# Filler bytes that shift where two tiles start in SBUF

## The chip, the cores and the metric

The kernel runs on one core of a Trainium2 chip. The metric is device time in microseconds (us) of one execution; the figure of a kernel is the median of its runs.

## The reference

The reference is two blocks of transformer-like layers on a sequence of 256 tokens with 1024 features, in float32. Each weight is used once, on all 256 tokens:

```python
for l in range(2):                     # first block
    h = hybrid_mixer(x, ...)           # x @ w_in (7680 columns), two attentions, a convolution, gates, w_mix_out
    x = layer_norm(alpha * x + h, ...)
    h = memory_cross_attention(x, mem, xa_q, xa_kv, xa_o)   # 256 memory tokens
    x = layer_norm(alpha * x + h, ...)
    h = conv_ffn(x, ...)               # x @ ffn_w_in (2 * 2816 columns), gating, @ ffn_w_out
    x = layer_norm(alpha * x + h, ...)
for l in range(2):                     # second block
    x = x + 0.5 * swiglu(norm(x), ...) # 1024 -> 2 * 2816 -> 1024
    x = x + mixer2(norm(x), ...)       # x @ w_in_2, two attentions, a convolution, a pooling, @ w_out_2
    x = x + 0.5 * swiglu(norm(x), ...)
```

## The kernel before, in words

All weights come from one packed array, in the order of use, as 674 halves of 128 x 1024 floats (512 KB). SP loads each into one of five staging tiles `stg`. A float32 product is made of three fast ones: ACT rounds the half to the format fp32r (`wh`, 8 buffers), DVE takes the rest `stg - wh` (`wl`, 7 buffers), the activations are split likewise, and TensorE adds high x high, low x high and high x low into PSUM. These products are nearly all of its work.

A TensorE product has a stationary operand of 128 x 128, which a weight load brings in, and a moving operand, which streams past it. There are three kinds of product here.

- `chunk_A`, lines 385 to 387: a piece of `wh` or `wl` is stationary, and 256 columns of activations move. The activations are `xT`, the normalised input of a layer transposed (8 chunks, high and low, 256 tokens; one tile, used by every layer), `memT`, the memory tokens in the same form, or pairs of 2 x 256 from `ring`.
- `group_B` and `group_Bt`, lines 423 to 425 and 445 to 452: a piece of `xT` or `memT` (128 tokens) is stationary, and 512 columns of `wh` or `wl` move.
- `run_BK`, lines 478 to 480 and 503: a piece of a `ring` pair is stationary, and 512 columns of `wh` or `wl` move. These are the projections at the end of each part.

The order is written out by hand: `weight_order` fixes the order of the halves, and the generator emits the instructions of side work (attention, convolution) between them. The change does not touch it.

Tiles lie in each of SBUF's 128 partitions one behind the other, pool after pool in the order in which the pools are made (`stg`, `wh`, `wl`, `one`, `xT`, a `gap`, `ring`, `tmp`, `sm`, and then those of `first`: `memT`, `KT` and small ones). Every tile is rounded up to 32 bytes. Only the first address of each pool is of interest here, taken modulo 256 bytes; all buffers of a pool and all slices that TensorE reads of these tiles are multiples of 256 bytes apart:

| tile | before | after |
|---|---|---|
| `stg`, `wh`, `wl` | 128 | 128 |
| `xT` | 32 | 64 |
| `ring`, `tmp` | 128 | 128 |
| `memT`, `KT` | 128 | 64 |
| `nab` (a mask, in attention) | 192 | 128 |

Quoted once, the pools around `xT`, in the kernel before:

```python
self.p_xT = P("xT", 1)
P("gap", 1).tile([128, 24], F32, name="gap")
self.p_ring = P("ring", 23)
```

Of the kernel before, what the change touches and what calls it, by code (L numbers as in the profile page):

```python
# [11 lines left out]
F32 = mybir.dt.float32  # L12
# [218 lines left out]
class Gen:  # L231
    def __init__(self, nc, tc, T, ctx):
        self.nc, self.tc, self.T, self.ctx = nc, tc, T, ctx
        P = lambda name, bufs, **k: ctx.enter_context(tc.tile_pool(name=name, bufs=bufs, **k))
        self.p_stg = P("stg", 5)
        self.p_hl = P("wh", NHL)
        self.p_wl = P("wl", NHL - 1)
        self.p_one = P("one", 1)
        self.p_xT = P("xT", 1)

        P("gap", 1).tile([128, 24], F32, name="gap")
        self.p_ring = P("ring", 23)
        self.p_tmp = P("tmp", 8)
        self.p_sm = P("sm", 24)
        PS = bass.MemoryType.PSUM
        self.p_acc = P("acc", 4, space=PS)
        self.p_tp = P("tp", 4, space=PS)
        self.used = 0
        self.n = 0
        self.cur = 0  # L250
        self.n_dma = 0
        self.n_h = 0
        self.n_l = 0
        self.stg = {}
        self.hl = {}
        self.lead = 4
        self.floor = None
        self.sides = []
        self.later = []
        self.early = []  # L260
# [556 lines left out]
    def setup(self):  # L817
        nc, T = self.nc, self.T
        one = self.p_one
        self.xn = one.tile([128, 2, D], F32, name="xn")  # L820
        self.ident = one.tile([128, 128], F32, name="ident")
        self.mhalf = one.tile([128, 8], F32, name="mhalf")
        self.cols = one.tile([128, N_COLS], F32, name="cols")
        self.lam = one.tile([128, DEPTH], F32, name="lam")
        self.subg = one.tile([128, DEPTH, 128], F32, name="subg")
        self.cs2 = one.tile([128, 2, 2, 16], F32, name="cs2")
        self.c1 = one.tile([128, 200], F32, name="c1")

    def first(self, ctx):
        nc, T = self.nc, self.T  # L830
        pf = ctx.enter_context(self.tc.tile_pool(name="first", bufs=1))
        pna = ctx.enter_context(self.tc.tile_pool(name="na", bufs=2))
        memT = pf.tile([128, 8, 2, 256], F32R, name="memT")
        KT = pf.tile([128, 8, 256], F32, name="KT")
        mraw = [self.ring([128, 2, 256]) for _ in range(4)]
        for k in range(4):
            nc.sync.dma_start(mraw[k], T["memT"][:, 2 * k:2 * k + 2, :])
            if k == 0:
                self.dma_w()
        for _ in range(3):  # L840
            self.dma_w()

        def load_x(t):
            for c in range(2):
                nc.sync.dma_start(self.halves(t)[c], T["x"][t * 128:t * 128 + 128, c * 512:c * 512 + 512])

        load_x(0)
        self.dma_w()
        g0, b0 = self.bcast_rows(T["emb_ln_g"], D, nc.sync), self.bcast_rows(T["emb_ln_b"], D, nc.sync)
        load_x(1)  # L850
        self.trig = pf.tile([128, 4, 2, 8], F32, name="trig")
        self.posf = pf.tile([128, 2], F32, name="posf")
        self.posi = pf.tile([128, 2], I32, name="posi")
        nc.gpsimd.memset(self.mhalf, -0.5)
        make_identity(nc, self.ident)
        self.memT, self.KT = memT, KT
        for k in range(4):
            self.split_to(memT[:, 2 * k:2 * k + 2, 0, :], memT[:, 2 * k:2 * k + 2, 1, :], mraw[k])
            if k == 0:
                self.pump(0, 0)  # L860

        def emb(t):
            list(self.ln_chain(self.halves(t), g0, b0))

        self.lead = 2
        self.xk(0, range(1))
        emb(0)
        nc.sync.dma_start(self.c1, T["c1"])
        nc.sync.dma_start(self.cols, T["cols"])
        lamr = self.lamr = self.ring([128, 2, 4, 64])  # L870
        nc.sync.dma_start(lamr, T["lamr"].partition_broadcast(128))
        nc.sync.dma_start(self.subg, T["subln_g"].partition_broadcast(128))
        nc.sync.dma_start(self.posi, T["pos"])
        self.xk(0, range(1, 2))
        xT = self.new_xT()
        self.transpose_in(0, self.halves(0), xT)
        self.lead = 3
        self.xk(0, range(2, 3))
        emb(1)
        self.lead = 4  # L880
        self.xk(0, range(3, 4))
        tr1 = self.turn1(self.halves(1), xT)
        for l in range(DEPTH):
            xT, tr1 = self.mixer1(l, xT, tr1, pna)
            xT, tr1 = self.cross(l, xT, tr1)
            if l == 0:
                self.sides.append(self.small_setup2())
            xT, tr1 = self.ffn1(l, xT, tr1)
        return xT, tr1
# [421 lines left out]
    def swiglu(self, l, which, xT, tr1, gap, final=False):  # L1311
# [21 lines left out]
        for j in range(2, NFF):  # L1333
            ps = self.chunk_A(("UG", n, l, j), x, pool=self.acc if j < NFF - 2 else self.tp)
            if j == 2:
                first()
            s, p = self.tmp([128, 256]), self.pair()
            nc.scalar.activation(s, ps[:, 1, :], AF.Silu)  # L1338
            nc.vector.tensor_tensor(s, ps[:, 0, :], s, op=ALU.mult)  # L1339
            self.split_to(p[:, 0, :], p[:, 1, :], s)  # L1340
            hT.append(p)
# [251 lines left out]
```

## Time and profile before

| | |
|---|---|
| median of 3 runs | 2063.93 us (2063.58 to 2064.59) |
| profiled execution, its own time | 2066.26 us |
| its span (first to last instruction) | 2064.5 us |
| PE, PEld busy | 99%, 90% |
| DVE, ACT busy | 63%, 53% |
| matmuls | 14064 |
| moved by DMA | 376.89 MB, 183 GB/s |

PE is TensorE's matmuls and PEld its weight loads; both overlap. The duration that the profile gives a matmul runs from its start to the end of its way through the array, and the next one starts long before that. What a matmul costs in a dense stretch is the distance from its start to the next start.

### The profile page before, as it was taken

What the parts mean: (1) busy time and instruction counts of PE and PEld (TensorE: products, weight loads), DVE (VectorE), ACT (ScalarE), POOL (GpSimd) and SP (SyncE); (2) the same over time, 40 slices, a digit from 0 to 9 for tenths busy, and PEclk for the clock granted to TensorE, in tenths of its full rate; (3) what the DMA queues carried; (4) which work ended last, traced back from release to release, by engine and by line L of the source; (5) the groups of instructions that cost most, each with busy time, mean ns of one, the idle gap of its engine ahead of it and who ended that gap; (6) DMA issues with size and microseconds to landing.
All of it is one profiled execution on the core that took longest, in us unless ns stands there. A gap on an engine that the chain in (4) does not pass through costs nothing.

```text
span 2064.5 us, 34809 instructions
## 1 busy us (share of the span) xinstructions
PE 2038.1 (99%) x14064; PEld 1864.0 (90%) x14064; DVE 1302.5 (63%) x2001; ACT 1091.1 (53%) x1798; POOL 96.8 (5%) x142
## 2 busy tenths in 40 slices
PE   8999999999999999999999999999999999999998
PEld 7899988899888999989987998879998998879996
DVE  6776674877577657457766555776555555676553
ACT  5757445465375644536553544575444544574442
POOL 2100000000010000000001000100000000100000
PEclk9999999999999999999999999999999999999999
DMA  7544664466564565545564656555564656545562
GB/s 287 189 152 164 200 215 137 144 208 200 184 204 135 172 205 175 190 136 187 187 240 158 205 184 223 159 160 174 184 220 147 206 187 222 162 152 179 186 216 72
DMA packets 105522, 376.89 MB, mean 183 GB/s; under 512 B 12560, under 2 KB 12816, under 8 KB 105232
## 3 DMA queue, kind: packets, MB, share of 16 engines
q1 hardware_dynamic: 99936, 357.85, 52.4%
q0 software_dynamic: 5136, 16.29, 2.9%
q8 instruction: 110, 1.80, 0.4%
q10 hardware_dynamic: 288, 0.52, 0.1%
q14 instruction: 52, 0.43, 0.1%
HBM read 372.49 MB, written 1.05 MB: 181 GB/s over the span
## 4 chain that ended last, share of the span: by engine, by line
PE 92%; DVE 4%; issue 1%; DMA 1%; POOL 1%; ACT 1%; SPq 0%; POOLq 0%; DVEq 0%
PE acc L385 17%; PE acc L386 16%; PE acc L387 16%; PE acc L480 6%; PE acc L478 6%; PE acc L479 6%; PE acc L503 4%; PE acc L423 3%; PE acc L425 3%; PE acc L424 3%; PE acc L452 1%; PE acc L447 1%; PE acc L445 1%; PE tp L387 1%; PE tp L385 1%
## 5 line engine op out<-in xcount | busy, mean ns | idle before, releaser
L320 DVE TENSOR_TENSOR wl<-stg,wh 128x1024 fp32r<-128x1024 f32 x670 | 801.5, 1223 | 187.8 <-PE acc L479 111.1
L308 ACT CAST wh<-stg 128x1024 fp32r<-128x1024 f32 (+1 forms) x673 | 683.9, 1047 | 177.2 <-PE acc L480 121.1
L385 PE MATMUL acc<-xT,wh 128*128 128x256 f32 x2624 | 740.7, 282 | 0.6 <-ACT xT L597 0.6
L386 PE MATMUL acc<-xT,wh 128*128 128x256 f32 x2624 | 736.2, 281 | 0.7 <-DVE xT L598 0.7
L387 PE MATMUL acc<-xT,wl 128*128 128x256 f32 x2624 | 736.1, 281 | 0.0
L385 PEld LDWEIGHTS acc<-xT,wh 128*128 128x128 f32 x2624 | 494.5, 188 | 3.3 <-ACT xT L597 1.1
L386 PEld LDWEIGHTS acc<-xT,wh 128*128 128x128 f32 x2624 | 494.6, 188 | 1.7 <-DVE xT L598 1.1
L387 PEld LDWEIGHTS acc<-xT,wl 128*128 128x128 f32 x2624 | 494.4, 188 | 0.0
L478 PE MATMUL acc<-wh,ring 128*128 128x512 f32 x528 | 207.3, 393 | 0.0
L480 PE MATMUL acc<-wh,ring 128*128 128x512 f32 x528 | 205.8, 390 | 0.2
L479 PE MATMUL acc<-wl,ring 128*128 128x512 f32 x528 | 205.6, 389 | 0.0
L480 PEld LDWEIGHTS acc<-wh,ring 128*128 128x128 f32 x528 | 99.1, 188 | 21.7 <-DVE ring L519 1.1
L478 PEld LDWEIGHTS acc<-wh,ring 128*128 128x128 f32 x528 | 99.1, 188 | 20.6 <-issue 0.3
L503 PE MATMUL acc<-wh,ring 128*128 128x512 f32 x384 | 117.5, 394 | 0.0
L479 PEld LDWEIGHTS acc<-wl,ring 128*128 128x128 f32 x528 | 99.2, 188 | 20.1
L1339 DVE TENSOR_TENSOR tmp<-acc,tmp 128x256 f32<-128x256 f32 x72 | 30.5, 424 | 137.2 <-ACT tmp L1338 137.2
L1338 ACT ACTIVATE tmp<-acc 128x256 f32<-128x256 f32 x72 | 27.7, 385 | 164.9 <-PE acc L387 164.9
L515 ACT CAST ring<-tmp 128x256 fp32r<-128x256 f32 x136 | 54.7, 407 | 87.2 <-DVE tmp L1246 42.0
L516 DVE TENSOR_TENSOR ring<-tmp,ring 128x256 fp32r<-128x256 f32 x136 | 57.3, 425 | 64.1 <-ACT ring L515 64.1
L503 PEld LDWEIGHTS acc<-wh,ring 128*128 128x128 f32 x384 | 72.1, 188 | 14.2
L539 POOL TENSOR_TENSOR sm<-sm,mhalf 128x1 f32<-128x1 f32 (+1 forms) x40 | 31.6, 790 | 1032.6 <-DVE sm L550 413.0
L423 PE MATMUL acc<-wh,xT 128*128 128x512 f32 (+1 forms) x192 | 75.3, 392 | 0.0
(235 smaller groups left out, 2649.7 us busy)
## 6 DMA issues: line engine op xcount, KB each, us to landing
stg<-in_wpack SPq DMA_DIRECT2D x673, 512.0 KB, 4.2
nab<-in_rpb POOLq DMA_DIRECT2D x8, 384.0 KB, 3.9
ring<-in_ln_g POOLq DMA_DIRECT2D x12, 256.0 KB, 3.7
ring<-in_ln_b POOLq DMA_DIRECT2D x12, 256.0 KB, 4.8
ring<-in_ffn_norm POOLq DMA_DIRECT2D x8, 256.0 KB, 4.3
cst<-hpad POOLq DMA_DIRECT2D x32, 32.9 KB, 4.1
ring<-in_memT SPq DMA_DIRECT2D x4, 256.0 KB, 5.5
xn<-in_x SPq DMA_DIRECT2D x4, 256.0 KB, 7.5
```

The lines of the kernel that those rows point to most:

```text
L308: self.nc.scalar.copy((h.bitcast(F32) if f32 else h)[:, c:c + w], self.stg[i][:, c:c + w])
L320: (self.nc.gpsimd if i in POOL_LOW else self.nc.vector).tensor_sub(l, s, self.hl[i][0].bitcast(F32))
L385: mm(out, lh, rh, start=start, stop=False)
L386: mm(out, lh, rl, start=False, stop=False)
L387: mm(out, ll, rh, start=False, stop=stop)
L423: mm(o, xp[:, 0, ts], h[:, w], start=(i == 0), stop=False)
L424: mm(o, xp[:, 0, ts], l[:, w], start=False, stop=False)
L425: mm(o, xp[:, 1, ts], h[:, w], start=False, stop=(i == n - 1))
L478: mm(b[t][c], xp[:, 0, ts], h[:, w], start=(i == 0), stop=False)
L479: mm(b[t][c], xp[:, 0, ts], l[:, w], start=False, stop=False)
L480: mm(b[t][c], xp[:, 1, ts], h[:, w], start=False, stop=False)
L503: mm(b[tt][cc], xp[:, 1 if kind == "x" else 0, ts], l[:, w] if kind[0] == "l" else h[:, w], start=False, stop=(kind == "x" and i == n - 1))
```

## The change

Four lines. The tile `c1` is made 32 bytes longer and used as before, which shifts `xT` by 32 bytes. The unused tile `gap` behind `xT` shrinks by 32 bytes, so that `ring` and all that follows it in the same pools stay where they are. A new unused tile `gap1` of 192 bytes ahead of `memT` shifts `memT`, `KT` and the small tiles behind them by 192 bytes. On each engine the same instructions stand in the same order, on tiles of the same names; only addresses differ.

```diff
--- before.py
+++ after.py
@@ -238,7 +238,7 @@
         self.p_one = P("one", 1)
         self.p_xT = P("xT", 1)
 
-        P("gap", 1).tile([128, 24], F32, name="gap")
+        P("gap", 1).tile([128, 16], F32, name="gap")
         self.p_ring = P("ring", 23)
         self.p_tmp = P("tmp", 8)
         self.p_sm = P("sm", 24)
@@ -824,12 +824,13 @@
         self.lam = one.tile([128, DEPTH], F32, name="lam")
         self.subg = one.tile([128, DEPTH, 128], F32, name="subg")
         self.cs2 = one.tile([128, 2, 2, 16], F32, name="cs2")
-        self.c1 = one.tile([128, 200], F32, name="c1")
+        self.c1 = one.tile([128, 208], F32, name="c1")[:, :200]
 
     def first(self, ctx):
         nc, T = self.nc, self.T
         pf = ctx.enter_context(self.tc.tile_pool(name="first", bufs=1))
         pna = ctx.enter_context(self.tc.tile_pool(name="na", bufs=2))
+        pf.tile([128, 48], F32, name="gap1")
         memT = pf.tile([128, 8, 2, 256], F32R, name="memT")
         KT = pf.tile([128, 8, 256], F32, name="KT")
         mraw = [self.ring([128, 2, 256]) for _ in range(4)]
```

## Rows read from the trace of the kernel before

**Rows 1.** The page: busy time, share of the span, instructions.

```profile
PE 2038.1 (99%) x14064; PEld 1864.0 (90%) x14064; DVE 1302.5 (63%) x2001; ACT 1091.1 (53%) x1798; POOL 96.8 (5%) x142
```

**Rows 2.** What PE waited for: total us, times, longest us.

```profile
PE acc L385 <- ACT wh L308: 5.4, 1, 5.4
...
PE acc L387 <- DVE wl L320: 2.4, 2, 1.9
...
PE acc L386 <- DVE xT L598: 0.7, 2, 0.3
PE acc L385 <- ACT xT L597: 0.6, 2, 0.3
...
PE acc L447 <- DVE wl L320: 0.3, 1, 0.3
PE acc L445 <- ACT xT L597: 0.2, 1, 0.2
```

**Rows 3.** Tile xT, its matmuls of 256 columns; duration in ns.

```profile
L385 PE MATMUL acc<-xT,wh x2624: 277/281/472, 47.5 to 1982.5; 128*128 128x256 f32 x188
...
L385 PE MATMUL tp<-xT,wh x192: 277/281/283, 490.6 to 1993.9; 128*128 128x256 f32 x192
```

**Rows 4.** Tile xT, matmuls that hold a piece of it.

```profile
L423 PE MATMUL acc<-wh,xT x192: 278/394/503, 72.3 to 1838.3; 128*128 128x512 f32 x160, 128*128 128x256 f32 x32
...
L445 PE MATMUL acc<-wh,xT x160: 388/394/793, 34.7 to 1875.9; 128*128 128x512 f32 x160
```

**Rows 5.** Tile memT, its matmuls, one row of three each.

```profile
L385 PE MATMUL acc<-memT,wh x128: 274/283/580, 5.4 to 875.8; 128*128 128x256 f32 x128
...
L423 PE MATMUL acc<-wh,memT x64: 387/389/582, 289.0 to 897.3; 128*128 128x512 f32 x64
```

**Rows 6.** Timeline of PE from 817.2 us, first and last of 15.

```profile
817.23 0.28 PE L385 MATMUL acc<-memT,wh 128*128 128x256 f32 x1
...
818.91 0.28 PE L387 MATMUL acc<-memT,wl 128*128 128x256 f32 x1
```

**Rows 7.** Windows in long stretches of xT: engines' busy us, instructions.

```profile
core 0: us, PE busy (x) PEld busy (x) DVE busy (x) ACT busy (x) POOL busy (x), PEclk, DMA share, GB/s
395.00:485.00 90.00, 90.00 (x761) 90.00 (x760) 69.54 (x128) 55.78 (x91) 0.58 (x1) 1.00 0.59 191
...
1610.00:1700.00 90.00, 90.00 (x770) 90.00 (x769) 50.98 (x66) 43.91 (x65) 0.00 (x0) 1.00 0.59 188
```

**Rows 8.** Timeline of PE from 316.8 us, first and last of 19.

```profile
316.77 0.28 PE L387 MATMUL acc<-xT,wl 128*128 128x256 f32 x1
...
318.93 0.28 PE L387 MATMUL acc<-xT,wl 128*128 128x256 f32 x1
```

**Rows 9.** A window in the down projection, ring as stationary operand.

```profile
1250.00:1300.00 50.00, 50.00 (x222) 41.39 (x222) 24.59 (x22) 19.91 (x20) 0.14 (x1) 1.00 0.70 227
```

**Rows 10.** Timeline of PE from 296.3 us, first and last of 12.

```profile
296.30 0.39 PE L425 MATMUL acc<-wh,memT 128*128 128x512 f32 x1
...
298.80 0.39 PE L424 MATMUL acc<-wl,memT 128*128 128x512 f32 x1
```

**Rows 11.** Timeline of PE from 1594.8 us, equal neighbours merged.

```profile
1594.80 1.79 PE L445 MATMUL acc<-wh,xT 128*128 128x512 f32 x7
1596.43 2.03 PE L447 MATMUL acc<-wl,xT 128*128 128x512 f32 x8
1598.30 1.09 PE L452 MATMUL acc<-wh,xT 128*128 128x512 f32 x4
```

**Rows 12.** Groups of PE by line: matmuls on the ring.

```profile
L478 PE MATMUL acc<-wh,ring 128*128 128x512 f32 x528 | 207.3, 393 | 0.0
...
L503 PE MATMUL acc<-wh,ring 128*128 128x512 f32 x384 | 117.5, 394 | 0.0
L503 PE MATMUL acc<-wl,ring 128*128 128x512 f32 x192 | 68.9, 389 | 0.0
...
L385 PE MATMUL acc<-ring,wh 128*128 128x256 f32 x192 | 54.7, 285 | 0.0
```

## The prediction

> **What bounds the kernel now.** I read the page first, then the waits of TensorE, then the matmuls by form, then the distance between the starts of neighbouring matmuls. The page gives PE 99% busy, PEld 90%, DVE 63%, ACT 53% [rows 1]. A busy PE is little evidence, since matmuls are pipelined; the waits say it better: what PE waits for other engines comes to 15.5 us of 2064.5 in ten rows from 5.4 to 0.2 [rows 2]. So the kernel lasts as long as 14064 matmuls take one behind the other, and the number to read is what one takes from its start to the next start, the slot. The duration of one (282 ns) is longer than its slot and isn't the cost.
>
> Seven matmuls in ten involve the tiles that move. 8448 matmuls stream 256 columns of xT past a 128x128 piece of wh or wl (3 x 2624 + 3 x 192) [rows 3]. 960 hold a piece of xT and stream 512 columns of wh or wl [rows 4]. memT does the same in 384 and 192 instructions [rows 5].
>
> **What the slots are.** The diff moves no instruction; it moves start addresses. So I look for places where one shape runs at different distances between its operands' addresses modulo 256 bytes. I write the distance as moving minus stationary.
> - Distance 0, 256 columns: memT against wh and wl. 14 slots between the two rows shown, 1.68 us, 120.0 ns each [rows 6].
> - Distance -96 (xT at 32, weights at 128): in six long stretches of several hundred matmuls a window of 90 us holds 761 of them (in four more windows 760 or 761) and 770 once [rows 7]. A window counts what overlaps it, so I divide 90.28 us by the count: 118.6 ns five times, 117.2 ns once. Same code, same data sizes, two patterns. A shorter stretch of cross attention ran a third one, 18 slots in 2.16 us, 120.0 ns [rows 8].
> - Distance 0, 512 columns: 50.39 us by 222 instructions, 227.0 ns (ring as stationary) [rows 9]; memT as stationary 11 slots in 2.50 us, 227.3 ns [rows 10].
> - Distance +96, 512 columns, xT as stationary: 7 slots in 1.63 us, then 8 in 1.87 us, 233.3 ns [rows 11].
>
> At distance 0 the second 256 columns cost 227 - 120 = 107 ns, 0.417 ns a column, which is 2.4 GHz; the granted clock in the windows was 1.00 of that [rows 7]. So 256 columns alone are 106.7 ns and every slot holds something more: 13.3 ns at distance 0 in both shapes (32 columns' time), 11.9 or 10.5 ns at -96, 20.0 ns at +96 (48 columns). 32 and 48 are two and three times 16 columns, and 16 columns of four bytes are 64 bytes. In the patterns at -96 the loss is 28.6 and 25.2 columns, about 1.8 and 1.6 of such pieces. My reading: while one stationary operand is loaded and another is streamed, the two reads meet a few times, and each meeting costs the time of 64 bytes. At a start that lies on 64 bytes (0) the count is whole and steady; at 32 bytes beside it (-96) it is broken and depends on how a stretch happened to begin.
>
> The Trainium skill speaks against this: "SBUF — State Buffer", section "SBUF: two separate sides", says that TensorE has ports of its own and never waits on anyone; "TensorE: Matmul & The Clock Gate", section "Step-by-step: what each phase is for", says that loading the next weights doesn't steal read bandwidth from the running matmul. By that rule the change is worth nothing and the time stays at 2063.9; by the rows, as summed below, it falls by 13. The trace disagrees with it at 120.0 against 117.2 ns and 227.0 against 233.3 ns for the same shapes.
>
> **The change part by part.**
> - xT goes from -96 to -64 as moving operand, from +96 to +64 as stationary one; memT and KT from 0 to -64. The ring's gap shrinks by what c1 and xT grew, so the ring, tmp and what lies behind stay where they were: 2160 slots of 227 ns on the ring as stationary operand (3 x 528 + 384 + 192) and 3 x 192 on it as moving one don't change [rows 12].
> - Nothing is added: the fillers are never written, c1 is still used as 200 columns. KT's 64 matmuls in scores and the writes of xT by ACT and DVE shift with their tiles; I put them at nothing, as PE's whole wait for xT is 1.5 us [rows 2], of which the shift could touch a part.
> - No row of before shows -64. Bounds for a 256-column slot: 106.7 ns (no meeting at all) and 126.7 ns (three meetings, as the 512-column rows at +96). For xT that is -95 to +74 us. Between them lie three plausible counts: 2 meetings, 120.0 ns, as at 0; 1.5, 116.7 ns; 1, 113.3 ns.
> - I take 1.5. Between 0 and -96 the count goes from 2 to 1.6 to 1.8, so it falls on this side of 0, and it rises on the other (3 at +96). A smooth curve through three points would put its low end near -64; a start on 64 bytes should also do away with the worse of the patterns.
>
> The sum. Long stretches of xT hold some 5700 of the 8448 matmuls; five of six run at 118.6 ns, so I count 4750 at 118.6 and 3700 at 117.2 (the short stretches show either).
> 4750 x (118.6 - 116.7) = 9.0 us; 3700 x (117.2 - 116.7) = 1.9 us; memT 384 x (120.0 - 116.7) = 1.3 us.
> 512 columns: +64 is two thirds of the way from 227.0 to 233.3, 231.2 ns: xT 960 x 2.1 = 2.0 us less, memT 192 x 4.2 = 0.8 us more.
> Together 9.0 + 1.9 + 1.3 + 2.0 - 0.8 = 13.4 us less. The profiled execution took 2066.26 us (span 2064.5), 2.3 above the median of 2063.93; the sum takes it to 2052.9, and a median to 2050.5. I say 2050.
>
> What has to keep up is hidden: in a window of 90 us DVE is busy 70 and ACT 56 at most [rows 7], so 1.6% more speed of PE finds weights split in time, and the DMA engines are at 0.6 there. If that cover were gone, PE would show waits for wl, which now come to 2.7 us [rows 2].
>
> **The rivals.**
> - No change that can be measured (the bound for this kernel is about 0.2%, 4.1 us): at -64 the same two patterns come up as at -96, or the start modulo 256 bytes doesn't matter and 117 against 120 has another cause, such as which instruction began the stretch. (By the Trainium skill's rule on the ports, above, it would be this case.) For it: three patterns appeared at one and the same distance. Only the 512-column rows give, about 1.2 us: 2062.
> - Slower: -64, lying on 64 bytes like 0, locks at two whole meetings, 120.0 ns. This is the third pattern that xT showed once. 4750 x 1.4 + 3700 x 2.8 = 17.0 us more, less 1.2: 2080. It decides from the point where the mean slot passes 118.1 ns, the mean of now. Against it: the loss falls from 0 towards -96.
> - Much faster: one meeting per slot, 113.3 ns. 4750 x 5.3 + 3700 x 3.9 = 39.6 us, memT 2.6, 512 columns 1.2: 43 less, 2021. Against it: no pattern seen goes below 117.2.
>
> **How the numbers follow.** Forecast (116 to 117.2 ns) 0.45, with a range of its own from 2043 to 2056; no change 0.25; slower 0.20; much faster 0.10. The range of 2034 to 2080 holds the forecast, no change and half of the slower case, and leaves out the much faster one. Faster by over 0.2%: 0.45 + 0.10 = 0.55; within: 0.25; slower: 0.20.
>
> **What the profile of the changed kernel would show.** Right: the same 90 us windows hold 773 matmuls or more, each of the six the same number; the slots of memT at 256 columns drop from 120.0 to those of xT; the ring's as stationary operand stay at 227.0; xT as stationary moves below 233.3. Wrong: memT still at 120.0 (distance doesn't matter, or -64 is as 0); 752 matmuls in a window (locked at 120.0); PE waiting for wl or wh by tens of us (the split no longer hidden).

## The result, and the profile after

The changed kernel takes 2031.62 us (median of 6 runs, 2028.78 to 2032.73), the kernel before 2064.14 in the same comparison (6 runs, 2063.58 to 2065.99): a ratio of 0.9839 [0.9826, 0.9852], 1.6% faster. The forecast was 2050 with a range from 2034 to 2080; the time is below the range. The profiled execution took 2029.3 us, 37.0 less in span than before (2064.5 to 2027.5).

The page of the changed kernel, its span and busy times; [rows 1] is the row of before:

```profile
span 2027.5 us, 34807 instructions
...
PE 1998.6 (99%) x14064; PEld 1827.9 (90%) x14064; DVE 1302.6 (64%) x2001; ACT 1090.8 (54%) x1798; POOL 97.8 (5%) x142
```

The instructions are the same, DVE and ACT are busy as long as before, and PE's share is the same 99%. Only PE's own time fell, by 39.5 us (2038.1 to 1998.6), and PEld's, its weight loads, with it. Now the windows of 90 us in the six long stretches of xT, and last the window on the ring, to be set beside [rows 7] and [rows 9]:

```profile
core 0: us, PE busy (x) PEld busy (x) DVE busy (x) ACT busy (x) POOL busy (x), PEclk, DMA share, GB/s
388.00:478.00 90.00, 90.00 (x797) 90.00 (x796) 72.42 (x132) 58.17 (x95) 0.58 (x1) 1.00 0.62 202
930.00:1020.00 90.00, 90.00 (x767) 90.00 (x766) 66.61 (x104) 55.71 (x88) 0.58 (x1) 1.00 0.60 191
1127.00:1217.00 90.00, 90.00 (x797) 90.00 (x796) 51.77 (x67) 44.52 (x68) 0.00 (x0) 1.00 0.62 198
1402.00:1492.00 90.00, 90.00 (x797) 90.00 (x796) 51.76 (x68) 44.74 (x67) 0.00 (x0) 1.00 0.63 198
1584.00:1674.00 90.00, 90.00 (x796) 90.00 (x796) 51.76 (x68) 44.80 (x67) 0.00 (x0) 1.00 0.62 199
1860.00:1950.00 90.00, 90.00 (x797) 90.00 (x796) 52.45 (x68) 45.46 (x67) 0.00 (x0) 1.00 0.62 197
1230.00:1280.00 50.00, 50.00 (x223) 41.40 (x222) 24.61 (x23) 19.93 (x21) 0.00 (x0) 1.00 0.70 226
```

Five stretches hold 796 or 797 matmuls where 761 or 770 stood: 90.28 / 797 = 113.3 ns a slot. The second holds 767: 117.7 ns, a pattern of its own, slower than the other five at the same distance. The granted clock is 1.00 in all, as before. The ring's window has 223 for 222, no change within one instruction at the edge. DVE is busy 72 of 90 us in the first window and 52 in the third, and the count is the same 797: how much DVE does beside a stretch is not what sets its slots.

Two timelines of PE. The first is memT with 256 columns (first and last of 20), beside [rows 6]:

```profile
803.79 0.28 PE L385 MATMUL acc<-memT,wh 128*128 128x256 f32 x1
...
805.95 0.28 PE L386 MATMUL acc<-memT,wh 128*128 128x256 f32 x1
```

19 slots in 2.16 us, 113.7 ns; it was 120.0. The second, xT as stationary operand with 512 columns, beside [rows 11]:

```profile
1567.75 2.00 PE L445 MATMUL acc<-wh,xT 128*128 128x512 f32 x8
1569.58 1.99 PE L447 MATMUL acc<-wl,xT 128*128 128x512 f32 x8
```

8 slots in 1.83 us, 228.8 ns; it was 233.3. The waits of PE (total us, times, longest us), beside [rows 2]:

```profile
PE tp L593 <- DVE tmp L575: 5.5, 2, 2.9
PE acc L385 <- ACT wh L308: 5.3, 1, 5.3
PE acc L387 <- DVE wl L320: 2.0, 1, 2.0
PE acc L447 <- DVE wl L320: 1.3, 1, 1.3
```

All waits together are 17.8 us for 15.5: about 2.3 us of the gain is given back in a layer's start (`tp`) and in waits for split weights.

**Where the 37 us come from.** I took the distances from each matmul's start to the next start from both traces (those under 150 ns for 256 columns, under 290 ns for 512), averaged them, and multiplied the change by the number of matmuls.

| matmuls | before | after | difference |
|---|---|---|---|
| 8448 of xT, 256 columns | 118.28 ns | 114.26 ns | -34.0 us |
| 960 of 512 columns, xT stationary | 233.4 | 229.4 | -3.8 |
| 384 of memT, 256 columns | 119.8 | 114.2 | -2.2 |
| 192 of 512 columns, memT stationary | 228.5 | 229.4 | +0.2 |
| more waiting of PE | | | +2.3 |

The sum is -37.5, against -37.0 in the spans.

### The profile page after: what moved, and what is told of

Read it like the earlier page. It is cut to its first block, busy times and chain, and to the rows that moved or that the text cites. A ratio compares the mean times of both kernels' runs of the same rounds, so it can differ in the third digit from the quotient of the medians.

```text
span 2027.5 us, 34807 instructions
## 1 busy us (share of the span) xinstructions
PE 1998.6 (99%) x14064; PEld 1827.9 (90%) x14064; DVE 1302.6 (64%) x2001; ACT 1090.8 (54%) x1798; POOL 97.8 (5%) x142
## 4 chain that ended last, share of the span: by engine, by line
PE 92%; DVE 4%; issue 1%; DMA 1%; POOL 1%; ACT 1%; SPq 0%; POOLq 0%; DVEq 0%
PE acc L385 16%; PE acc L386 16%; PE acc L387 16%; PE acc L480 6%; PE acc L478 6%; PE acc L479 6%; PE acc L503 4%; PE acc L423 3%; PE acc L425 3%; PE acc L424 3%; PE acc L452 1%; PE acc L447 1%; PE acc L445 1%; PE tp L387 1%; PE tp L385 1%
## 5 line engine op out<-in xcount | busy, mean ns | idle before, releaser
L385 PE MATMUL acc<-xT,wh 128*128 128x256 f32 x2624 | 732.0, 279 | 0.6 <-ACT xT L597 0.6
L386 PE MATMUL acc<-xT,wh 128*128 128x256 f32 x2624 | 727.2, 277 | 0.7 <-DVE xT L598 0.7
L387 PE MATMUL acc<-xT,wl 128*128 128x256 f32 x2624 | 726.9, 277 | 0.0
L503 PE MATMUL acc<-wh,ring 128*128 128x512 f32 x384 | 117.5, 394 | 0.0
L1339 ACT ACTIVATE tmp<-acc 128x256 f32<-128x256 f32 x72 | 27.8, 386 | 148.5 <-PE acc L387 148.5
```

What stands on the lines that cost most here:

```text
L385: mm(out, lh, rh, start=start, stop=False)
L386: mm(out, lh, rl, start=False, stop=False)
L387: mm(out, ll, rh, start=False, stop=stop)
L503: mm(b[tt][cc], xp[:, 1 if kind == "x" else 0, ts], l[:, w] if kind[0] == "l" else h[:, w], start=False, stop=(kind == "x" and i == n - 1))
```

## The experiments

All are edits of the changed kernel, on the lines of its fillers. `xT` distance below is the start of xT minus the start of the weights, modulo 256 bytes: the moving minus the stationary operand for 256 columns, the reverse for 512. Where nothing else is said, memT stays at -64 and the ring at 0. Ratios are to the kernel before, timed on the same chip. The window shown is 80 us of the first long stretch, so a slot there is 80.28 us by its count; its columns are those of the windows above.

### One part alone

e_xT_only drops memT's filler (memT at 0 as before, xT at -64):

```diff
-        pf.tile([128, 48], F32, name="gap1")
```

> xT alone at -64 from the weights, memT and KT left at distance 0. If the slot depends on the distance of the two operands of that very matmul: xT's 256-column slots are 113.3 or 117.8 ns as after the change, memT's go back to 120.0 and, as stationary operand, to 227; against the changed kernel 384 x 5.7 ns = 2.2 us more and 192 x 2 ns = 0.4 us less, some 2033. If the mask or the small tiles that moved with memT had the gain: near 2064.

Measured: 2026.20 us (2 runs, 2023.73 and 2028.67), 0.9809 [0.978, 0.9838].

```profile
395.00:475.00 80.00, 80.00 (x709) 80.00 (x708) 65.09 (x120) 51.75 (x85) 0.58 (x1) 1.00 0.61 201
```

e_mem_only takes xT back to -96 and keeps memT at -64:

```diff
-        P("gap", 1).tile([128, 16], F32, name="gap")
+        P("gap", 1).tile([128, 24], F32, name="gap")
-        self.c1 = one.tile([128, 208], F32, name="c1")[:, :200]
+        self.c1 = one.tile([128, 200], F32, name="c1")[:, :200]
```

> memT, KT and the small tiles moved alone, xT left at -96. If distance decides: xT keeps its 118.6 and 117.2 ns, memT alone goes from 120.0 to 113.3 and its 512-column slots from 227 to 229; 2064 less 2, some 2062. If the small tiles carried the gain: near 2032.

Measured: 2064.50 us (8 runs), 0.9994 [0.9983, 1.0006]; memT's slots are 113.6 ns, xT's 118.7 or 117.3 as before.

```profile
395.00:475.00 80.00, 80.00 (x677) 80.00 (x676) 62.16 (x118) 50.51 (x83) 0.58 (x1) 1.00 0.57 191
```

So the gain is xT's. memT's part, 2.0 us by the table above, is real in its slots (113.6 ns) and too small for these runs to show in the time.

### Other distances of xT

Each moves xT by the length of `c1` and closes the difference with `gap`, so that the ring stays at its distance. The first, level with the weights:

```diff
-        P("gap", 1).tile([128, 16], F32, name="gap")
-        self.c1 = one.tile([128, 208], F32, name="c1")[:, :200]
+        self.c1 = one.tile([128, 224], F32, name="c1")[:, :200]
```

> xT at distance 0 from the weights (128 modulo 256 as they are), all else as in the changed kernel. If distance decides: xT's 256-column slots are a steady 120.0 ns as memT's were, its 512-column slots 227; against before 8448 x 1.7 = 14.5 us more, 960 x 6.4 = 6.1 less, memT 2 less: 2070. If what counts is that the tile begins on a multiple of 64 bytes, wherever the weights are: 113.3 ns and 2032, as 128 is one too.

```profile
395.00:475.00 80.00, 80.00 (x669) 80.00 (x668) 62.02 (x117) 49.78 (x82) 0.58 (x1) 1.00 0.58 190
```

e_plus64, with `c1` of 240 and `gap` of 48:

> xT at distance +64 (192 modulo 256). If distance modulo 256 decides: the other side of 0, where the 512-column rows lost three pieces at +96; 256-column slots at 120 ns or more, up to 126.7, so 2070 to 2130. If the pattern repeats after 128 bytes, or if a start on 64 bytes is all that counts: as at -64, 113.3 ns and 2032.

```profile
395.00:475.00 80.00, 80.00 (x681) 80.00 (x681) 62.67 (x119) 50.85 (x84) 0.58 (x1) 1.00 0.58 193
```

e_minus32 (`c1` 216, `gap` 8), e_plus32 (232, 56), e_minus128 (256, 32) and e_plus96 (248, 40):

> xT at -32 (96 modulo 256). Seen so far for xT's 256-column slots: 118.7 and 117.3 ns at -96, 113.3 and 117.8 at -64, 120.0 at 0, 117.8 at +64. If the loss is smooth in the distance: between -64 and 0, 116 to 118 ns, and 512-column slots 228; 2045 to 2062. If a start off the 64-byte grid gives broken counts (as -96 did): 117.3 and 118.7 ns in a mixture, 2056 to 2062.

> xT at +32 (160 modulo 256). If the pattern repeats after 128 bytes, +32 is the same as -96: 118.7 and 117.3 ns at 256 columns and 233 ns at 512, 2064. If it repeats only after 256 bytes and is smooth: between 0 (120.0) and +64 (117.8), 119 ns and 2068.

> xT at -128 (0 modulo 256), on the 64-byte grid. If the pattern repeats after 128 bytes: 120.0 ns and 227 as at distance 0, 2075. If after 256 bytes: it lies between -96 and +96, some other count; by a smooth curve 117 to 119 ns, 2050 to 2066.

> xT at +96 (224 modulo 256). If the pattern repeats after 128 bytes: the same as -32 in the run beside this one. If after 256 bytes: unlike it, and by a smooth curve between +64 (117.8 ns) and -96 (118.3), some 2062. As stationary operand it is then at -96 from the moving weights: 256-column rows at that distance lost less than at 0, so 512 columns below 227 if roles don't matter.

The windows of e_plus32, the fastest of the four, and of e_plus96, the slowest of all:

```profile
395.00:475.00 80.00, 80.00 (x688) 80.00 (x687) 63.41 (x119) 51.08 (x85) 0.58 (x1) 1.00 0.61 194
```

```profile
395.00:475.00 80.00, 80.00 (x669) 80.00 (x668) 62.07 (x117) 49.72 (x82) 0.58 (x1) 1.00 0.58 188
```

e_minus48 and e_minus80 leave the grid of 32 bytes: the tile of xT is 32 bytes longer and its data begin 16 bytes in (e_minus48 with `gap` of 8; e_minus80 with `c1` of 200 and `gap` as it is):

```diff
-        return self.p_xT.tile([128, 8, 2, 256], F32R, tag="xT", name=self.nm("xT"))
+        t = self.p_xT.tile([128, 4104], F32R, tag="xT", name=self.nm("xT"))
+        return t[:, 4:4100].rearrange("p (a b c) -> p a b c", a=8, b=2)
```

> xT at -48, half way between -64 (113.3 and 117.8 ns) and -32 (118.3). If -64 is a narrow spot: 117 to 118.5 ns, 2052 to 2066. If the loss goes on from -64 in a line: 116 ns, 2045.

> xT at -80, half way between -96 (118.7 and 117.3 ns) and -64. With -48 at 119.2 ns, -64 looks like a narrow spot: here too 117 to 119 ns, 2055 to 2066, if a start must lie on 64 bytes from the weights; 115 to 116 ns and 2045 if it is a slope on this side.

```profile
395.00:475.00 80.00, 80.00 (x673) 80.00 (x673) 62.11 (x117) 49.77 (x82) 0.58 (x1) 1.00 0.60 192
```

The window is that of e_minus80; e_minus48's is the next.

```profile
395.00:475.00 80.00, 80.00 (x674) 80.00 (x673) 61.98 (x116) 49.73 (x83) 0.58 (x1) 1.00 0.59 191
```

All of them together, with the loss over 106.7 ns counted in columns' times of 0.417 ns. The 256-column slot is that of the long stretches; only at +32 is the second value that of some shorter ones, and at -48 four shorter ones ran at 116.7 ns. The 512-column slot is the average over xT's slots, taken as in the table above.

| xT distance | kernel | 256 columns, ns | loss, columns | 512 columns, ns | median us | ratio |
|---|---|---|---|---|---|---|
| -128 | e_minus128 | 118.7 | 28.8 | 232.4 | 2067.39 | 1.0016 [1.0005, 1.0027] |
| -96 | before | 118.6 or 117.2 | 28.6 or 25.2 | 233.4 | 2064.14 | 1 |
| -80 | e_minus80 | 119.3 | 30.2 | 230.2 | 2071.03 | 1.0026 [1.0014, 1.0038] |
| -64 | after | 113.3 or 117.8 | 15.8 or 26.6 | 229.4 | 2031.62 | 0.9839 [0.9826, 0.9852] |
| -48 | e_minus48 | 119.2 | 30.0 | 232.5 | 2069.96 | 1.002 [1.0008, 1.0031] |
| -32 | e_minus32 | 118.3 | 27.8 | 233.1 | 2064.98 | 1.0001 [0.999, 1.0012] |
| 0 | e_level | 120.0 | 31.9 | 228.8 | 2075.37 | 1.0046 [1.0026, 1.0066] |
| +32 | e_plus32 | 116.7 or 117.8 | 24.0 or 26.6 | 233.2 | 2052.98 | 0.9948 [0.9925, 0.997] |
| +64 | e_plus64 | 117.8 | 26.6 | 233.3 | 2060.35 | 0.9974 [0.9962, 0.9985] |
| +96 | e_plus96 | 120.0 | 31.9 | 234.0 | 2079.13 | 1.0075 [1.0053, 1.0098] |

There is no curve through these. -64 stands alone: 16 bytes to either side cost the whole gain (2071 and 2070), and the next best, +32, is on the other side of 0. The distance that is lowest for 512 columns, 0 (228.8 ns, against 229.4 at -64), is among the worst for 256.

### Is it the distance, or where the tile lies?

e_all32 shifts everything by 32 bytes, weights included; all distances are those of the changed kernel, and xT no longer starts on a multiple of 64 bytes. e_plus192 moves xT on by another 256 bytes (`c1` of 272, `gap` as it is):

```diff
+        P("pad", 1).tile([128, 8], F32, name="pad")
```

> The changed kernel with 32 more bytes ahead of everything: weights at 160, xT and memT at 96, ring at 160 modulo 256; every distance as after the change, but no tile begins on a multiple of 64 any more. If distance decides: 113.3 and 117.8 ns for xT, 2026 to 2033. If a start on 64 bytes counts: broken counts as at -96, 117 to 119 ns, 2050 to 2066.

> xT another 256 bytes further on, at distance +192, all else as in the changed kernel. If the pattern repeats after 256 bytes: as after the change, 113.3 and 117.8 ns, 2026 to 2033. If it repeats after 512 bytes or more: something else, by the spread of the other distances 117 to 120 ns and 2050 to 2080.

Measured: e_all32 2028.72 us (2 runs), 0.982 [0.9791, 0.9848]; e_plus192 2028.34 us (2 runs), 0.9818 [0.9789, 0.9846]. Their windows, in this order:

```profile
395.00:475.00 80.00, 80.00 (x708) 80.00 (x707) 65.12 (x120) 51.73 (x86) 0.58 (x1) 1.00 0.61 202
```

```profile
395.00:475.00 80.00, 80.00 (x709) 80.00 (x708) 65.11 (x120) 51.78 (x86) 0.58 (x1) 1.00 0.62 202
```

Both run the 113.3 ns pattern here; their second long stretch runs at 117.8 ns, as in the changed kernel. So it is the distance between the two operands that counts, not the tile's own address, and at -64 it repeats after 256 bytes. It doesn't repeat after 128: +64 is not -64.

### Which operand meets which

The three products of one chunk (lines 385 to 387) hold `wh`, `wh` and `wl`. e_wl_level puts `wl` level with xT (distance 0) and leaves `wh` at -64 from it:

```diff
+        P("padw", 1).tile([128, 48], F32, name="padw")
-        self.c1 = one.tile([128, 208], F32, name="c1")[:, :200]
+        self.c1 = one.tile([128, 224], F32, name="c1")[:, :200]
```

> wl alone moved, to distance 0 from xT (64 modulo 256), wh still at -64. Lines 385, 386, 387 hold wh, wh, wl; while 386 streams, wl is loaded for 387. If a slot grows by the load that runs beside it, 386 grows from 113.3 to some 120 ns and 387 stays; if by the stationary operand that it uses itself, 387 grows and 386 stays; if both, no one of them stands out. Mean of the three near 115.6 ns, 8448 x 1.3 = 11 us more than after the change, 2040; the ring's 512-column slots, whose moving wl is then at -64, some 229 in one of three, 2 us more.

Measured: 2067.01 us (8 runs), 1.0008 [0.9996, 1.0019]. The expectation fell.

```profile
395.00:475.00 80.00, 80.00 (x682) 80.00 (x681) 62.70 (x119) 50.66 (x83) 0.58 (x1) 1.00 0.61 192
```

80.28 / 682 = 117.7 ns, and none of the three lines stands out (118.2, 118.1 and 117.5 ns from their starts to the next, over the trace; `wl` is the last). At line 385 `wh` is held, and the load beside it is of `wh` too, both at -64; yet it lost the gain like the others. So the slots can't be priced one by one by the addresses that meet in them: one operand in three at another distance takes the gain from all three. The time holds a little more than that, since `wl` moved against the other tiles too: over the trace, xT's 256-column slots make 30.8 of the 37.8 us by which the span grew, and the ring's 512-column slots, up from 227.0 to 229.7 ns, another 5.8.

e_half_level asks whether the weight load has a share in it. It starts from e_level (all slots 120.0 ns) and loads only 64 of the 128 columns of `wl`; it leaves out half of the low x high product:

```diff
-        mm(out, lh, rl, start=False, stop=False)
-        mm(out, ll, rh, start=False, stop=stop)
+        mm(out[:64], ll[:, :64], rh, start=False, stop=False)
+        mm(out, lh, rl, start=False, stop=stop)
```

> xT at distance 0 (a steady 120.0 ns and 2075 us so far); in the 256-column products of chunk_A the low weights are taken second and only 64 of their 128 columns are loaded, which leaves out half of that small product. Line 386 holds the short load; it is loaded while 385 streams. If the load beside a stream costs the stream 16 columns' time each time that they meet: 385 falls from 120.0 to some 113.3 ns, 386 and 387 stay; some 2056. If the extra 13.3 ns belong to a matmul's own stationary operand: 386 falls. If neither: all stay at 120.0 and 2075.

Measured: 2046.43 us (2 runs), 0.9909 [0.9891, 0.9927], 28.9 below e_level.

```profile
395.00:475.00 80.00, 80.00 (x688) 80.00 (x687) 62.86 (x116) 50.27 (x84) 0.58 (x1) 1.00 0.61 196
```

The mean slot falls from 120.0 to 116.7 ns, although every matmul still streams 256 columns. That points to the load having a share in what a stream takes, but doesn't show it: the edit also swaps the last two products, and the short one writes half the rows; neither was run by itself. None of the cases that were expected came: the fall is larger and spread over the lines, to 116.4 (beside the short load), 114.9 (the product of the short load) and 118.75 ns.

### The two fastest again

> The changed kernel once more, beside the one with xT alone moved: each run has its own share of 113.3 and 117.8 ns stretches, and a long stretch at 117.8 instead of 113.3 costs 816 x 4.4 ns = 3.6 us, so runs in clusters some 3.6 us apart, 2025 to 2033.

> xT alone at -64, memT at 0. If memT's place matters only for memT: 2 us slower than the changed kernel at equal shares of the two patterns, 2027 to 2035. If memT's place also helps xT's stretches into the quicker pattern: some 4 us faster, as the first run was (2026 against 2032).

Measured: 2027.36 us (4 runs, 2023.08 to 2028.01), 0.9812 [0.9799, 0.9825], and 2029.11 us (5 runs, 2024.67 to 2030.86), 0.982 [0.9807, 0.9834]: the same within their spread, so memT's filler can't be told from nothing. No version ran that beats the changed kernel for certain. In the first one the slow stretch is another: here the first long stretch of after_again, which ran at 113.3 ns in the execution shown above:

```profile
395.00:475.00 80.00, 80.00 (x681) 80.00 (x680) 62.16 (x115) 49.82 (x84) 0.58 (x1) 1.00 0.61 195
```

80.28 / 681 = 117.9 ns; its other five run at 113.3. A long stretch has 910 to 934 slots in the trace (not the 816 of the expectation), and 4.4 ns more on each is 4.0 to 4.1 us. The times of single runs lie about that far apart (2023.1, 2027.2 to 2028.0; 2024.7, 2028.0 to 2030.9). The profiled executions bear it out: those with one slow long stretch took 2028.0 to 2030.6 us, and the one in which none was slow, that of e_xT_only, took 2023.7. Its second long stretch, slow in the changed kernel:

```profile
930.00:1015.00 85.00, 85.00 (x752) 85.00 (x752) 65.81 (x103) 55.16 (x86) 0.58 (x1) 1.00 0.61 200
```

85.28 / 752 = 113.4 ns. For the runs without a profile it stays worked out.

## Why the prediction was wrong

- **The bound and the number to read** were right. PE runs without a pause, and the change is in its slots: 34.0 of the 37 us are xT's 256-column slots. DVE's and ACT's busy times moved by 0.3 us at most, and the ring's slots stayed.
- **The mechanism** was right in part: the address distance modulo 256 bytes decides which slots come up (e_all32, e_plus192, e_level), and the loss at -64 is 15.8 columns, close to the time of 64 bytes. That the loss comes from the load beside the stream, that the two reads *meet*, and that each meeting costs 64 bytes' time is not shown: e_half_level points to the load, with the two side changes named there, and most losses in the table are no whole number of 16 columns.
- **The step that failed** is "I take 1.5", with its reason, "A smooth curve through three points would put its low end near -64". Measured, the count is 1 in five long stretches (113.3 ns) and 1.67 in one (117.7 ns), 114.26 ns over all of xT's slots where the sum had 116.7; that is 20.6 us of the 23.6 by which the fall was put too small. The much faster rival, put at 0.10, named this pattern. The bounds of the sum, 106.7 and 126.7 ns, did hold every value measured; choosing inside them by interpolation was the error. The table has no smooth curve: -80 and -48 cost 119 ns, against 113.3 between them.
- **Against it stood** "no pattern seen goes below 117.2". Only two distances had been seen for 256 columns, so it said little about a third.
- **"At a start that lies on 64 bytes (0) the count is whole and steady"** fell, whether the tile's start or the distance is meant: e_all32 has no tile on that grid and runs as fast, while the distance +64 lies on it with 26.6 columns and -64 has two patterns itself. "The same 90 us windows hold 773 matmuls or more, each of the six the same number" was right for five and wrong for one.
- **The much faster rival's 43 us** against the 37.0 measured: its xT term, 39.6, came to 34.0 (the one long stretch at 117.8 ns costs 4.1, shorter stretches like it and the starts of stretches cost more; the mean before was 118.28 ns, not the 118.0 of the prediction's split, which gives a part back); its 512-column term, 1.2, came to 3.6 net (xT at 229.4 ns for the 231.2 that the prediction read off a straight line); and PE waits 2.3 us more.
- **The cover** held: DVE is busy 72 us of 90 in the fastest window, and waits for `wl` at lines 387 and 447 are 3.3 us for 2.7.
- **The Trainium skill's rule** that TensorE never waits on anyone ("SBUF — State Buffer", section "SBUF: two separate sides") would have given 2063.9. The runs disagree: the same instructions in the same order took from 2026 to 2079 us by addresses alone.

**What stays open.** What decides in which pattern a stretch runs: at -64 most stretches settle on 113.3 ns and some on 117.8, and which ones differs from execution to execution of one kernel. Why one `wl` in three at distance 0 spoils all three slots: a slot that shifts the next one's load against its stream would do it, but no run isolates that. Whether the load beside a stream is the cause of the loss at all.

## What to carry to other kernels

Where TensorE is 99% busy and waits for nothing, read the distance from start to start of one form and compare it between places and executions: more than one value for one shape is time that waiting for other engines doesn't explain. The distance between the starts of the moving and the stationary tile, modulo 256 bytes, moved this kernel by 53 us (medians of 2026 to 2079) with no instruction changed. It is cheap to sweep with unused bytes. Here it had to be swept in steps of 16 or 32 bytes, since interpolating failed, and the one try at giving `wh` and `wl` different distances lost the gain. The best distance may depend on the product: for 256 moving columns it was -64, for 512 no distance that was measured was quicker than 0 (227.0 ns in the ring's slots, 228.8 in xT's).

## What the hardware showed that I had not expected

- How narrow the good distance is: 113.3 ns in most long stretches at -64, 119.3 at -80, 119.2 at -48.
- What counts is moving minus stationary, whichever tile plays which part. In the few 256-column products in which `wh` or `wl` moves and a piece of xT is held (96 of them), the sign turns: they take 114.1 ns with xT at +64 and 116.7 with xT at -64. At each of the eight distances whose opposite was run too, they lie within 1.2 ns of a value that xT's own stretches show at the opposite distance.
- A stretch settles in its first few slots, and stays so. The timeline of PE in the changed kernel, at the start of a long stretch:

```profile
1397.34 0.28 PE L386 MATMUL acc<-xT,wh 128*128 128x256 f32 x1
1397.45 0.28 PE L387 MATMUL acc<-xT,wl 128*128 128x256 f32 x1
1397.57 0.28 PE L385 MATMUL acc<-xT,wh 128*128 128x256 f32 x1
1397.69 0.28 PE L386 MATMUL acc<-xT,wh 128*128 128x256 f32 x1
1397.81 0.28 PE L387 MATMUL acc<-xT,wl 128*128 128x256 f32 x1
1397.93 0.28 PE L385 MATMUL acc<-xT,wh 128*128 128x256 f32 x1
1398.04 0.28 PE L386 MATMUL acc<-xT,wh 128*128 128x256 f32 x1
1398.15 0.28 PE L387 MATMUL acc<-xT,wl 128*128 128x256 f32 x1
1398.27 0.28 PE L385 MATMUL acc<-xT,wh 128*128 128x256 f32 x1
1398.38 0.28 PE L386 MATMUL acc<-xT,wh 128*128 128x256 f32 x1
1398.49 0.28 PE L387 MATMUL acc<-xT,wl 128*128 128x256 f32 x1
```

From 1397.34 to 1397.93 five slots take 0.59 us, 118 ns each; the next five take 0.56, 112 ns by these rounded starts. Of the 18 stretches of over 90 slots in this trace, 15 are at 113 ns in slots 6 to 10 and stay there; the other three are at 118 then and stay there to their ends, the slow long one among them.
